# A two-layer encoder: four instead of three seven-product tiles per second matrix, and an adding DMA for their sums

## The chip, the cores and the metric

The kernel runs on one core of one Trainium2 chip. The metric is the device time of one execution in microseconds (us), as the median of several runs; lower is better. The engines are named as in the profile: PE (matmul), PEld (its weight loads), DVE (VectorE), ACT (ScalarE), POOL (GpSimd), SP (SyncE, which here only issues DMAs).

## The reference, cut to what matters

A trunk of two layers on 256 tokens of width 2048, float32. Each layer is an attention (which the change does not touch) and a squared-ReLU MLP with 8192 hidden units, each added to a residual `x`.

```python
def sq_relu_mlp(h, w1, w2):
    return jnp.square(jax.nn.relu(h @ w1)) @ w2      # w1: 2048 x 8192, w2: 8192 x 2048

for i in range(DEPTH):                               # DEPTH = 2
    ...                                              # x = x + attention(rms_norm(x))
    x = x + sq_relu_mlp(rms_norm(x, g), w1, w2)
return rms_norm(x, final_norm)
```

## The kernel before

**Accuracy by parts.** Every float32 operand is cut into a high part (float32r, made by ACT with a cast) and a low part (the rest, made by DVE with a subtraction). One product of two 128-row blocks is three matmuls of 128x512 (high by high, high by low, low by high; lines 196 to 198). The parts of the weights are the tiles `wh` and `wl` (`split`, lines 191 and 192).

**The MLP in groups.** Each of the two MLPs runs in four groups of 2048 hidden units (`ffn`, g = 0 to 3). A group is four calls of `gemm_pair`: two column pairs (cp = 0 and 1) of the first matrix, then two of the second. A column pair multiplies 256 rows by 2048 by 1024 columns. It is eight *steps*; a step takes one pair of 128-row tiles of the left side and one weight block of 512 KB twice (two DMAs on SP's queue).

**Two kinds of step.** An "s" step does the usual eight products (24 matmuls). An "x" step does seven (21 matmuls), by a Strassen-like scheme: DVE first makes sums of the four weight blocks (`prep_x`: tile `sums`, and one block of `w` overwritten), ACT and DVE cut these into `hs` and `ls`, and the left side needs sums of its own, which `sums_and_parts` makes on DVE for each hidden tile pair in `pairs2`. Four of the seven products go into extra PSUM banks ("1", "6", "7", "5"); after the last x step of a column pair, in its last step, `begin` combines them in an SBUF tile `C` (128 x 4 x 512).

**Order of the work.** The order of each engine is the order in which the program is written, step by step; nothing is moved afterwards. While PE multiplies step i, ACT and DVE make the parts of step i+2 (`prep(i + 2, n)` behind quarter n of the step: sums at n = 0, parts of the first half at n = 1, `ls` at n = 2, parts of the second half at n = 3). The pool of `wh` and `wl` has four buffers and a step uses two of each, so the parts of step i+2 go into the buffers of step i and cannot be made earlier than PE lets go of them. Weights are loaded three to five steps ahead into three buffers.

**Between the matrices.** In the second step behind a column pair of the first matrix (for cp = 1 that is the second step of the second matrix), PE transposes the squared hidden values in four rounds r = 0 to 3, each into one of the four extra PSUM banks; ACT and DVE empty each bank into `hT` (a pair not in `pairs2`: cast by ACT, subtraction by DVE at line 192; a pair in `pairs2`: a copy by ACT at line 702, and `sums_and_parts` in a later step). The first x step of the next column pair writes these same banks.

**The residual.** For the second matrix, `put` adds the four standard banks to `x` in the last step (DVE, four of 128x512 from PSUM). `early` adds what stands in `C` to `x` on DVE (one of 128x1024 and two of 128x512) in two later steps of the next column pair, for groups 0 to 2; in group 3 it stands in the last step or near it, because the next norm needs `x`.

The order of the eight steps of a second-matrix column pair, with `pairs2 = (2, 3, 5)`, is s0 s1 x2 s4 x3 s6 x5 s7 in groups 0 to 2.

Of the kernel before, what the change touches and what calls it, by code (L numbers as in the profile page):

```python
# [14 lines left out]
P = 128  # L15
# [32 lines left out]
def tile_encoder(ctx: ExitStack, tc: tile.TileContext, ins, out):  # L48
# [84 lines left out]
    def subtract(engine, out, a, b):  # L133
        engine.tensor_tensor(out=out, in0=a, in1=b, op=ALU.subtract)  # L134
# [143 lines left out]
    QUARTERS = (0, 0), (1, 0), (1, 1), (0, 1)  # L278
    STD = {(0, 0): "2", (0, 1): "3", (1, 0): "4", (1, 1): "S"}

    def gemm_pair(w, cp, A, sums_of, order, finish, split_end=False):
        made, q = [], {}
        first_x = [n for n, o in enumerate(order) if o[0] == "x"]
        touched = set()

        def left(pair, which):

            t, u = A[pair // 2], 2 * (pair % 2)
            if which in ("S2", "S3", "S4"):
                c = sums_of[pair]  # L290
                return [c[:, h, ("S3", "S2", "S4").index(which), :] for h in range(2)]
            a, ts_ = {"A11": (0, 0), "A12": (1, 0), "S1": (0, 1), "A21": (0, 1), "A22": (1, 1)}[which]
            return [t[:, u + a, h, ts_ * P:(ts_ + 1) * P] for h in range(2)]

        def product(bank, a, b, last):
            if not q:
                q.update({k: banks[:, n, :] for k, n in sum_banks().items()})
            three(q[bank], a, b, bank not in touched, last)
            touched.add(bank)

        X = (("1", "A11", 2), ("2", "A12", 3), ("6", "S2", 6), ("7", "S3", 4), ("4", "A22", 0), ("3", "S4", 1),
             ("5", "S1", 5))

        for n, (kind, pair) in enumerate(order):
            k, u = pair // 2, pair % 2
            loads = [(w[k, 2 * cp + c].rearrange("p (a n) -> p a n", n=512)[:, 2 * u:2 * u + 2, :],
                      2 - 2 * c, 4 - 2 * c) for c in (1, 0)]
            if kind == "x":
                def quarter(s, m, pair=pair, n=n):
                    for bank, a, b in X[2 * m:2 * m + 2]:  # L310
                        product(bank, left(pair, a), (s.hi[b], s.lo[b]), n == first_x[-1] and bank in "1567")
            else:
                def quarter(s, m, pair=pair, n=n):
                    tb, c = QUARTERS[m]
                    for kk in range(2):
                        b = 2 * (1 - c) + kk
                        a = (("A11", "A12"), ("A21", "A22"))[tb][kk]
                        product(STD[tb, c], left(pair, a), (s.hi[b], s.lo[b]), n == len(order) - 1 and kk == 1)
            s = Step(kind, loads, quarter)
            s.even = pair % 2 == 0  # L320
            steps.append(s)
            made.append(s)

        if split_end:
            ends = made[-2:]
            for e, s in enumerate(ends):
                def quarter(s, m, e=e):
                    tb, m = m // 2, m % 2
                    pair = order[len(order) - 2 + m][1]
                    for kk in range(2):  # L330
                        b = 2 * (1 - e) + kk
                        a = (("A11", "A12"), ("A21", "A22"))[tb][kk]
                        product(STD[tb, e], left(pair, a), (ends[m].hi[b], ends[m].lo[b]), m == 1 and kk == 1)
                s.quarters = quarter

        def begin(m):
            if m == 0:
                C = q["C"] = part.pool.tile([P, 4, 512], F32, name="C", tag="C")
                nc.scalar.copy(C[:, 0, :], q["1"])
                subtract(nc.vector, C[:, 1, :], q["6"], C[:, 0, :])  # L340
            elif m == 1:
                subtract(nc.vector, q["C"][:, 2, :], q["C"][:, 1, :], q["7"])
            elif m == 2:
                add(nc.vector, q["C"][:, 1::2, :], q["C"][:, 1:3, :], q["5"].unsqueeze(1).to_broadcast([P, 2, 512]))

        s = made[first_x[-1] + 1]
        for m in range(3):
            s.after[0 if s is made[-1] else m].append(lambda m=m: begin(m))
        finish(made, q)
        return made  # L350
# [317 lines left out]
    def ffn(norm, w1, w2, next_norm, next_done):  # L668
        for g in range(4):
            last = g == 3  # L670
            pairs2 = (3, 5) if last else (2, 3, 5)
            hT, sums = [None] * 4, {}

            def hidden(made, q, cp, hT=hT, sums=sums, pairs2=pairs2, last=last):
# [10 lines left out]
                for r in range(4):  # L685
# [10 lines left out]
                    def post(r=r, held=held):  # L696
                        c, half, pair = 2 * cp + r // 2, r % 2, 4 * cp + r
                        if half == 0:
                            hT[c] = opool.tile([P, 4, 2, T], F32R, name="hT", tag="o")
                        if pair in pairs2:  # L700
                            raw = part.pool.tile([P, 2, T], F32, name="h", tag="h", bufs=2)
                            nc.scalar.copy(raw, held["t"])

                            def parts_of(c=c, half=half, raw=raw, pair=pair):
                                sums[pair] = part.pool.tile([P, 2, 3, P], F32R, name="hs", tag="hsum", bufs=3)
                                sums_and_parts(raw, hT[c], half, sums[pair])
                            steps[i + (3 if cp else 2 * r - 1)].after[1].append(parts_of)
                        else:
                            to = hT[c][:, 2 * half:2 * half + 2]
                            split(to[:, :, 0, :], to[:, :, 1, :], held["t"])  # L710
# [11 lines left out]
            def residual(made, q, cp, parted, last=last):  # L722
# [1 line left out]
                    add(nc.vector, to(cp, tb, c), to(cp, tb, c), q[STD[tb, c]])  # L724

                def early(n):
                    C = q["C"]
                    if n == 0:
                        o = x[:, 0, cp * 1024:(cp + 1) * 1024]
                        add(nc.vector, o, o, C[:, 0:2, :].rearrange("p a n -> p (a n)"))  # L730
                    else:
                        subtract(nc.vector, to(cp, 1, 0), to(cp, 1, 0), C[:, 2, :])
                        add(nc.vector, to(cp, 1, 1), to(cp, 1, 1), C[:, 3, :])

                if not parted:
                    i = steps.index(made[-1])
                    for n in range(2):
                        if last:
                            made[-1].after[n].append(lambda n=n: early(n))
                        else:  # L740
                            at_after(i + 4 + 2 * n, 1, lambda n=n: early(n))
                    for m, (tb, c) in enumerate(QUARTERS):
                        made[-1].after[m].append(lambda tb=tb, c=c: put(tb, c))
                    if last:
# [20 lines left out]

            for cp in range(2):
                parted = last and cp == 1
                order = range(8) if last else (0, 1, 2, 4, 3, 6, 5, 7)
                if parted:
                    order = ((0, 1, 2, 4, 3, 5, 6, 7), (0, 1, 3, 2, 5, 4, 6, 7))[next_done is None]  # L770
                gemm_pair(w2g, cp, hT, sums, ff_order(pairs2, order), lambda made, q, cp=cp, parted=parted: residual(made, q, cp, parted),
                          parted)

    ffn(norms[1], ins["ffn0_w1"], ins["ffn0_w2"], lambda: norms[2], begin_norm(2, True))

# [360 lines left out]
```

## Time and profile before

| | |
|---|---|
| median of 3 runs | 2272.35 us (2272.34 to 2273.08) |
| the profiled execution | 2271.95 us, of which the span is 2270.2 us |
| PE busy | 2247.7 us (99%), 10904 matmuls |
| DVE busy | 1876.2 us (83%), 2215 instructions |
| ACT busy | 1263.4 us (56%), 1570 instructions |
| POOL busy | 0.7 us, 6 instructions |
| granted TensorE clock | 0.999 |
| HBM read | 426.38 MB, 189 GB/s over the span |

How to read it: the span runs from the first to the last instruction of the program; the remaining 1.75 us of the execution lie around it. The busy share of an engine is a mean over the attention and the MLPs. In the views "lines", a row is a group of like instructions: source line, engine, operation, tiles out<-in with their shapes, count, then the summed and mean duration, then the idle time of the engine just before them and what ended it. Consecutive instructions of one engine overlap a little, so the distance from start to start, not the duration, is what an instruction occupies; matmuls of 128x512 have a duration of about 0.39 us but follow each other at about 0.227 us.

### The profile page before, as it was taken

How to read it: one execution, taken by the hardware profiler on the slowest of the kernel's cores; microseconds unless marked ns; L12 is line 12 of the kernel's file. 1: busy time of each engine (PE TensorE's matmuls, PEld its weight loads, DVE VectorE, ACT ScalarE, POOL GpSimd, SP SyncE). 2: the span in 40 equal slices, each digit the busy share in tenths (PEclk: the TensorE clock that was granted, in tenths of full speed). 3: DMA queues.
4: the chain of work that ended last, by engine and by line, in shares of the span. 5: the costliest groups of instructions: out<-in, count | busy, mean ns of one | idle time of the engine just before them, and what ended most of it. 6: DMA issues, size and time to landing. Idle time of an engine off the chain costs nothing.

```text
span 2270.2 us, 28396 instructions
## 1 busy us (share of the span) xinstructions
PE 2247.7 (99%) x10904; PEld 1883.7 (83%) x10904; DVE 1876.2 (83%) x2215; ACT 1263.4 (56%) x1570; POOL 0.7 (0%) x6
## 2 busy tenths in 40 slices
PE   8999999999999999999999999999999999999998
PEld 7888888888888888888888888888888888888886
DVE  6777666899999999989877667757999999999988
ACT  6555445665565565565444544456665665664664
POOL 0000000000000000000000000000000000000000
PEclk9999999999999999999999999999999999999999
DMA  7556555556656656655555445544666666656664
GB/s 252 185 177 190 181 178 175 186 186 205 203 186 203 205 185 198 206 179 189 204 176 182 180 167 170 182 168 149 205 198 196 199 193 197 203 189 201 199 214 143
DMA packets 110728, 430.33 MB, mean 190 GB/s; under 512 B 23872, under 2 KB 24448, under 8 KB 92160
## 3 DMA queue, kind: packets, MB, share of 16 engines
q1 hardware_dynamic: 109920, 426.82, 58.0%
q10 hardware_dynamic: 672, 1.70, 0.2%
q8 instruction: 85, 1.39, 0.2%
q14 instruction: 51, 0.42, 0.1%
HBM read 426.38 MB, written 2.10 MB: 189 GB/s over the span
## 4 chain that ended last, share of the span: by engine, by line
PE 91%; DVE 5%; ACT 2%; issue 1%; DMA 0%; SPq 0%; ACTq 0%; DVEq 0%
PE banks L196 23%; PE banks L198 23%; PE banks L197 23%; PE banks L221 13%; PE banks L223 7%; DVE wl L192 2%; PE banks L693 1%; DVE C L137 1%; DVE sums L137 1%; DVE C L134 0%; ACT wh L191 0%; PE banks L379 0%; ACT hs L177 0%; ACT C L679 0%; PE banks L891 0%
## 5 line engine op out<-in xcount | busy, mean ns | idle before, releaser
L192 DVE TENSOR_TENSOR wl<-w,wh 128x1024 fp32r<-128x1024 f32 (+1 forms) x802 | 965.8, 1217 | 294.3 <-ACT wh L191 288.8
L191 ACT CAST wh<-w 128x1024 fp32r<-128x1024 f32 (+1 forms) x802 | 829.6, 1048 | 583.1 <-PE banks L198 338.5
L221 PE MATMUL banks<-xT,wh 128*128 128x512 f32 x1280 | 456.4, 400 | 0.0
L196 PE MATMUL banks<-wh,xT 128*128 128x512 f32 x1104 | 434.9, 394 | 0.0
L198 PE MATMUL banks<-wh,xT 128*128 128x512 f32 x1104 | 430.1, 390 | 0.0
L197 PE MATMUL banks<-wl,xT 128*128 128x512 f32 x1104 | 430.0, 390 | 0.0
L223 PE MATMUL banks<-xT,wl 128*128 128x256 f32 x1280 | 359.0, 280 | 0.0
L196 PE MATMUL banks<-wh,hT 128*128 128x512 f32 x804 | 316.3, 393 | 1.9 <-DVE hT L192 1.9
L198 PE MATMUL banks<-wh,hT 128*128 128x512 f32 x804 | 313.2, 390 | 0.0
L197 PE MATMUL banks<-wl,hT 128*128 128x512 f32 x804 | 313.0, 389 | 0.0
L221 PEld LDWEIGHTS banks<-xT,wh 128*128 128x128 f32 x1280 | 241.2, 188 | 55.8
L198 PEld LDWEIGHTS banks<-wh,xT 128*128 128x128 f32 x1104 | 207.2, 188 | 43.8
L223 PEld LDWEIGHTS banks<-xT,wl 128*128 128x128 f32 x1280 | 242.3, 189 | 0.2
L196 PEld LDWEIGHTS banks<-wh,xT 128*128 128x128 f32 x1104 | 207.4, 188 | 41.0
L197 PEld LDWEIGHTS banks<-wl,xT 128*128 128x128 f32 x1104 | 207.6, 188 | 40.6
L177 ACT CAST hs<-sums 128x1536 fp32r<-128x1536 f32 x92 | 136.6, 1485 | 180.2 <-DVE sums L137 180.2
L196 PEld LDWEIGHTS banks<-wh,hT 128*128 128x128 f32 x804 | 151.0, 188 | 33.3 <-DVE hT L192 3.3
L198 PEld LDWEIGHTS banks<-wh,hT 128*128 128x128 f32 x804 | 150.9, 188 | 31.8
L197 PEld LDWEIGHTS banks<-wl,hT 128*128 128x128 f32 x804 | 151.1, 188 | 30.1
L134 DVE TENSOR_TENSOR ls<-sums,hs 128x1536 fp32r<-128x1536 f32 x92 | 161.1, 1751 | 0.3 <-ACT hs L177 0.3
L137 DVE TENSOR_TENSOR sums<-w 128x1024 f32<-128x1024 f32 x92 | 112.1, 1218 | 0.0
L196 PE MATMUL banks<-wh,oT 128*128 128x512 f32 x192 | 76.5, 399 | 0.0
(188 smaller groups left out, 2289.3 us busy)
## 6 DMA issues: line engine op xcount, KB each, us to landing
w<-in_ffn_w_dram SPq DMA_DIRECT2D x512, 512.0 KB, 4.7
w<-in_dil_wqkv_dram SPq DMA_DIRECT2D x72, 1024.0 KB, 4.8
w<-in_na_wqkv_dram SPq DMA_DIRECT2D x47, 1024.0 KB, 4.9
w<-in_na_wo_dram SPq DMA_DIRECT2D x16, 1024.0 KB, 4.8
w<-in_dil_wo_dram SPq DMA_DIRECT2D x8, 1024.0 KB, 4.7
bias<-in_rpb_dram SPq DMA_DIRECT2D x32, 96.0 KB, 9.9
out_dram<-x SPq DMA_DIRECT2D x8, 256.0 KB, 2.6
x<-in_x_dram SPq DMA_DIRECT2D x3, 512.0 KB, 9.3
```

The lines of the kernel that those rows point to most:

```text
L134: engine.tensor_tensor(out=out, in0=a, in1=b, op=ALU.subtract)
L137: engine.tensor_tensor(out=out, in0=a, in1=b, op=ALU.add)
L177: nc.scalar.copy(s.hs, s.sums)
L191: nc.scalar.copy(dst_hi, src)
L192: nc.vector.tensor_tensor(out=dst_lo, in0=src, in1=dst_hi.bitcast(F32), op=ALU.subtract)
L196: nc.tensor.matmul(o, left[0], right[0], start=start, stop=False)
L197: nc.tensor.matmul(o, left[0], right[1], start=False, stop=False)
L198: nc.tensor.matmul(o, left[1], right[0], start=False, stop=stop)
L221: nc.tensor.matmul(o, s.hi[a][:, cs], xt.rearrange("p h t -> p (h t)"), start=first, stop=False)
L223: nc.tensor.matmul(o[:, :T], s.lo[a][:, cs], xt[:, 0, :], start=False, stop=last)
L693: nc.tensor.transpose(t[:, a, tb * P:(tb + 1) * P], q["C"][:, 2 * tb + f // 4, f % 4 * P:(f % 4 + 1) * P], ident)
```

## The change

In groups 0 to 2 of both MLPs the second matrix gets a fourth pair by seven products (`pairs2 = (2, 3, 5, 6)`), a fourth buffer for the sums of the left side, and other orders: s0 s1 x2 x3 s4 x5 x6 s7 for cp = 0 and s0 x2 x3 s1 x5 s4 x6 s7 for cp = 1. `sums_and_parts` for the hidden pairs 5 and 6 stand in the fourth and fifth step of cp = 0 (before: pair 5 in the fourth). The two `early` additions of these groups go from DVE; in their place one DMA, issued by POOL in the first step of the next column pair, adds the whole of `C` to `x` in SBUF. So that one addition serves all four blocks, `begin` stores its third block negated (`negated=True`, for all second matrices), which makes three DVE instructions into four.

```diff
-    def gemm_pair(w, cp, A, sums_of, order, finish, split_end=False):
+    def gemm_pair(w, cp, A, sums_of, order, finish, split_end=False, negated=False):
...
             elif m == 1:
-                subtract(nc.vector, q["C"][:, 2, :], q["C"][:, 1, :], q["7"])
+                ab = (q["7"], q["C"][:, 1, :]) if negated else (q["C"][:, 1, :], q["7"])
+                subtract(nc.vector, q["C"][:, 2, :], *ab)
+            elif m == 2 and negated:
+                C = q["C"]
+                subtract(nc.vector, C[:, 3, :], q["5"], C[:, 2, :])
+                add(nc.vector, C[:, 1, :], C[:, 1, :], q["5"])
...
-            pairs2 = (3, 5) if last else (2, 3, 5)
+            pairs2 = (3, 5) if last else (2, 3, 5, 6)
...
-                                sums[pair] = part.pool.tile([P, 2, 3, P], F32R, name="hs", tag="hsum", bufs=3)
+                                sums[pair] = part.pool.tile([P, 2, 3, P], F32R, name="hs", tag="hsum", bufs=4)
                                 sums_and_parts(raw, hT[c], half, sums[pair])
-                            steps[i + (3 if cp else 2 * r - 1)].after[1].append(parts_of)
+                            steps[i + (2 + r if cp else 2 * r - 1)].after[1].append(parts_of)
...
                 def early(n):
-                    C = q["C"]
-                    if n == 0:
-                        o = x[:, 0, cp * 1024:(cp + 1) * 1024]
-                        add(nc.vector, o, o, C[:, 0:2, :].rearrange("p a n -> p (a n)"))
-                    else:
-                        subtract(nc.vector, to(cp, 1, 0), to(cp, 1, 0), C[:, 2, :])
-                        add(nc.vector, to(cp, 1, 1), to(cp, 1, 1), C[:, 3, :])
+                    o = x[:, n, cp * 1024:(cp + 1) * 1024]
+                    add(nc.vector, o, o, q["C"][:, 2 * n:2 * n + 2, :].rearrange("p a n -> p (a n)"))
+
+                def bring():
+                    nc.gpsimd.dma_start(x[:, :, cp * 1024:(cp + 1) * 1024],
+                                        q["C"].rearrange("p (t a) n -> p t (a n)", t=2), accum_op=ALU.add)
 
                 if not parted:
                     i = steps.index(made[-1])
-                    for n in range(2):
-                        if last:
+                    if last:
+                        for n in range(2):
                             made[-1].after[n].append(lambda n=n: early(n))
-                        else:
-                            at_after(i + 4 + 2 * n, 1, lambda n=n: early(n))
+                    else:
+                        at_after(i + 1, 1, bring)
...
-                order = range(8) if last else (0, 1, 2, 4, 3, 6, 5, 7)
+                order = range(8) if last or not cp else (0, 2, 3, 1, 5, 4, 6, 7)
...
                 gemm_pair(w2g, cp, hT, sums, ff_order(pairs2, order), lambda made, q, cp=cp, parted=parted: residual(made, q, cp, parted),
-                          parted)
+                          parted, negated=True)
```

Where this moves DVE's instructions, first place: the last step of cp = 0 of a second matrix, group 0. Before, the combining of `C`, the four additions to `x`, and the parts of an s step (two `wl`) stand here, and the next step's x sums follow:

```order
L134 TENSOR_TENSOR C<-banks,C 128x512
L134 TENSOR_TENSOR C<-C,banks 128x512
L137 TENSOR_TENSOR C<-C,banks 128x2x512
L137 TENSOR_TENSOR x<-x,banks 128x512 x2
L192 TENSOR_TENSOR wl<-w,wh 128x1024
L137 TENSOR_TENSOR x<-x,banks 128x512 x2
L192 TENSOR_TENSOR wl<-w,wh 128x1024
L137 TENSOR_TENSOR sums<-w 128x1024
```

In the changed kernel the same step holds the preparation of an x step (three additions into `sums` and `w`, two `wl`, one `ls`), laid between the additions to `x`:

```order
L134 TENSOR_TENSOR C<-banks,C 128x512 x3
L137 TENSOR_TENSOR C<-C,banks 128x512
L137 TENSOR_TENSOR x<-x,banks 128x512
L137 TENSOR_TENSOR sums<-w 128x1024
L137 TENSOR_TENSOR sums<-sums,w 128x512
L137 TENSOR_TENSOR w<-sums,w 128x512
L137 TENSOR_TENSOR x<-x,banks 128x512
L192 TENSOR_TENSOR wl<-w,wh 128x1024
L137 TENSOR_TENSOR x<-x,banks 128x512
L134 TENSOR_TENSOR ls<-sums,hs 128x1536
L137 TENSOR_TENSOR x<-x,banks 128x512
L192 TENSOR_TENSOR wl<-w,wh 128x1024
```

So x2 of cp = 1 is prepared one step earlier, in the step that also ends cp = 0.

Second place: DVE in the second step of cp = 0 of a second matrix, where the transposed hidden values are emptied from their banks (`hT<-banks`). Before, behind the last `wl` of x2's preparation (first row), the emptying of round 0 comes at once, between the parts of an s step:

```order
L192 TENSOR_TENSOR wl<-w,wh 128x1024
L192 TENSOR_TENSOR hT<-banks,hT 128x2x256
L192 TENSOR_TENSOR wl<-w,wh 128x1024
L192 TENSOR_TENSOR hT<-banks,hT 128x2x256 x2
L192 TENSOR_TENSOR wl<-w,wh 128x1024
L137 TENSOR_TENSOR sums<-w 128x1024
L137 TENSOR_TENSOR sums<-sums,w 128x512
```

In the changed kernel the sums of x3 stand ahead of it:

```order
L192 TENSOR_TENSOR wl<-w,wh 128x1024
L137 TENSOR_TENSOR sums<-w 128x1024
L137 TENSOR_TENSOR sums<-sums,w 128x512
L137 TENSOR_TENSOR w<-sums,w 128x512
L192 TENSOR_TENSOR hT<-banks,hT 128x2x256
L192 TENSOR_TENSOR wl<-w,wh 128x1024
L134 TENSOR_TENSOR ls<-sums,hs 128x1536
L192 TENSOR_TENSOR hT<-banks,hT 128x2x256
L192 TENSOR_TENSOR wl<-w,wh 128x1024 x3
```

What moved: three additions now stand between x2's last `wl` and the first `hT<-banks`, and of the three emptyings by DVE two are left (round 2 is now a copy by ACT).

## The prediction

> **What bounds the kernel now.** I read the page first, then the windows of one group, then DVE's timeline step by step. The page's busy line:
>
> ```profile
> PE 2247.7 (99%) x10904; PEld 1883.7 (83%) x10904; DVE 1876.2 (83%) x2215; ACT 1263.4 (56%) x1570; POOL 0.7 (0%) x6
> ```
>
> PE is busy throughout, so fewer matmuls are worth time. But 83% for DVE is a mean over attention and MLPs. Here are four windows from the second group of the first MLP on: cp = 0 and cp = 1 of a second matrix, then cp = 0 and cp = 1 of the next first matrix; the columns are the window's length, then busy time of PE, PEld, DVE, ACT, POOL.
>
> ```profile
> 658.92:703.37 44.45, 43.88 (x201) 35.88 (x200) 41.13 (x47) 28.68 (x34) 0.00 (x0) 1.00 0.62 194
> 703.37:744.85 41.48, 41.48 (x185) 34.36 (x184) 38.42 (x39) 21.51 (x20) 0.00 (x0) 1.00 0.67 213
> 744.85:786.33 41.48, 41.48 (x185) 34.36 (x184) 38.43 (x39) 21.49 (x20) 0.00 (x0) 1.00 0.64 199
> 786.33:829.90 43.57, 43.57 (x200) 35.81 (x199) 40.44 (x48) 29.57 (x36) 0.00 (x0) 1.00 0.58 183
> ```
>
> DVE works 41.13 of 44.45 us where the change adds to it: 3.3 us are free there, and 3.1 in the next window. The clock is full (1.00). What matters then is how far DVE may fall behind PE. I cut PE's stream into steps of 24 or 21 matmuls; the first three of cp = 0:
>
> ```profile
> 658.92:664.36 5.44, 5.44 (x25) 4.50 (x24) 5.44 (x8) 4.50 (x6) 0.00 (x0) 1.00 0.54 189
> 664.36:672.77 8.41, 7.84 (x42) 6.08 (x41) 6.83 (x8) 6.99 (x10) 0.00 (x0) 1.00 0.42 125
> 672.77:677.53 4.76, 4.76 (x22) 3.89 (x23) 4.73 (x6) 2.72 (x4) 0.00 (x0) 1.00 0.72 229
> ```
>
> An s step takes 5.44 us (24 matmuls, 0.227 each), an x step 4.76 (21), and the second step 8.41 because it holds the transposes. Now DVE's timeline from the parts of s1 to the emptying of the first transposes (start, duration, line, operation, and in brackets idle time before it):
>
> ```profile
> 662.60 1.22 DVE L192 TENSOR_TENSOR wl<-w,wh 128x1024 fp32r<-128x1024 f32 x1
> 663.74 1.22 DVE L137 TENSOR_TENSOR sums<-w 128x1024 f32<-128x1024 f32 x1
> 664.99 0.69 DVE L137 TENSOR_TENSOR sums<-sums,w 128x512 f32<-128x512 f32 x1
> 665.72 0.69 DVE L137 TENSOR_TENSOR w<-sums,w 128x512 f32<-128x512 f32 x1
> 666.33 1.22 DVE L192 TENSOR_TENSOR wl<-w,wh 128x1024 fp32r<-128x1024 f32 x1
> 667.46 1.75 DVE L134 TENSOR_TENSOR ls<-sums,hs 128x1536 fp32r<-128x1536 f32 x1
> 670.73 1.23 DVE L192 TENSOR_TENSOR wl<-w,wh 128x1024 fp32r<-128x1024 f32 x1 [1.51 <-ACT wh L191]
> 671.87 0.68 DVE L192 TENSOR_TENSOR hT<-banks,hT 128x512 fp32r<-128x512 f32 x1
> 672.47 1.22 DVE L192 TENSOR_TENSOR wl<-w,wh 128x1024 fp32r<-128x1024 f32 x1
> ```
>
> By starts, an x step's preparation occupies DVE for 2.59 (three additions) + 1.13 + 1.67 (`ls`, 1.75 less 0.08 of overlap) + 1.14 = 6.53 us, against 4.76 to 5.44 of PE's time; an s step's takes two `wl`, 2.27. I call *lag* how long after the end of PE's step i DVE ends its work of that step. The work of the step that ends at 658.92 ends at 663.82: lag 4.9. The preparation of x2 ends at 671.96, and its PE step at 664.36: lag 7.6. No PE stall follows, because the step between is 8.41 long. So DVE already trails PE by about a step, and only x-free stretches bring it back. How much lag is allowed shows in PE's rows of x2:
>
> ```profile
> 672.61 0.50 PE L196 MATMUL banks<-wh,hT 128*128 128x512 f32 x1 [0.31 <-DVE hT L192]
> ...
> 674.34 0.39 PE L197 MATMUL banks<-ls,hs 128*128 128x512 f32 x1
> ```
>
> PE first needs `ls` 1.73 us into the x step, and behind `ls` DVE has one more `wl` (1.14): the lag may reach the length of the step between plus some 2.7 us, so 7.4 before an x step that follows an x step, 8.1 when an s step lies between. The other two tiles of the step (`wl` at once and `wl` in the second half) give 0.2 more.
>
> **The change part by part.** Removed from PE: two column pairs x three groups x two MLPs = 12 x steps in place of s steps, 3 matmuls each: 36 x 0.227 = 8.2 us, all on the path (PE 99%). That is 1.36 us a group, for six groups.
>
> Added to DVE per group: two x preparations for s ones, 2 x (6.53 - 2.27) = 8.5 us; one `sums_and_parts` for one emptying of 0.60 (671.87 to 672.47). This is its cost, from its first to its last instruction and the next one:
>
> ```profile
> 682.46 0.28 DVE L134 TENSOR_TENSOR c<-h 128x128 f32<-128x128 f32 x1
> ...
> 685.26 2.36 DVE L192 TENSOR_TENSOR wl<-w,wh 128x1024 fp32r<-128x1024 f32 x2 [0.29 <-ACT wh L191]
> ```
>
> 2.5 us, 2.8 with the wait for ACT behind it: +1.9. The combining of `C`, the additions to `x`, and the idle time ahead of them:
>
> ```profile
> 698.53 1.22 DVE L192 TENSOR_TENSOR wl<-w,wh 128x1024 fp32r<-128x1024 f32 x1 [0.98 <-ACT wh L191]
> 699.67 0.68 DVE L134 TENSOR_TENSOR C<-banks,C 128x512 f32<-128x512 f32 x1
> 700.39 0.69 DVE L134 TENSOR_TENSOR C<-C,banks 128x512 f32<-128x512 f32 x1
> 701.18 1.22 DVE L137 TENSOR_TENSOR C<-C,banks 128x1024 f32<-128x1024 f32 x1
> 702.32 1.28 DVE L137 TENSOR_TENSOR x<-x,banks 128x512 f32<-128x512 f32 x2
> 703.51 1.22 DVE L192 TENSOR_TENSOR wl<-w,wh 128x1024 fp32r<-128x1024 f32 x1
> 704.65 1.27 DVE L137 TENSOR_TENSOR x<-x,banks 128x512 f32<-128x512 f32 x2
> 705.85 1.22 DVE L192 TENSOR_TENSOR wl<-w,wh 128x1024 fp32r<-128x1024 f32 x1
> ```
>
> Combining takes 2.65 and, as four instructions of 128x512, 0.72 + 0.79 + 0.72 + 0.60 = 2.83; the four additions 2.39. The 0.98 us idle is DVE waiting for buffers that PE still holds: the lag cannot fall under the 1.8 us that this row leaves (699.75 against 697.93, where PE's x5 ends: 677.53 and two s and two x steps).
>
> Taken from DVE: the `early` additions, twice per group.
>
> ```profile
> 723.25 1.22 DVE L137 TENSOR_TENSOR x<-x,C 128x1024 f32<-128x1024 f32 x1
> 724.38 1.22 DVE L192 TENSOR_TENSOR wl<-w,wh 128x1024 fp32r<-128x1024 f32 x1
> ...
> 733.45 0.68 DVE L134 TENSOR_TENSOR x<-x,C 128x512 f32<-128x512 f32 x1
> 734.05 0.68 DVE L137 TENSOR_TENSOR x<-x,C 128x512 f32<-128x512 f32 x1
> 734.65 3.86 DVE L192 TENSOR_TENSOR wl<-w,wh 128x1024 fp32r<-128x1024 f32 x3
> ```
>
> 1.13 + 1.20 = 2.33, twice 4.7 us. Net, DVE gets 8.5 + 1.9 + 0.4 - 4.7 = 6.1 us more per group. But the relief lies in the middle of cp = 1 and in the next first matrix, where DVE waits for buffers anyway; the load lies in cp = 0 and at the seam to cp = 1. So I follow the lag through the steps (after each: lag + work - PE's step).
>
> Step s0 is as before: lag 7.6. Step s1: the sums of x3 now stand ahead of the first `hT<-banks`. The row at 672.61 shows that x2's first product waits for exactly that instruction (the bank of round 0), so PE now waits 2.59 us more: **first stall 2.6**. The step becomes 11.0 long; work 6.53 + 2 x 0.60: lag 7.6 + 7.7 - 11.0 = 4.3. Step x2: + 2.27 - 4.76 = 1.8, the floor. Step x3 (prepares x5, with pair 5's `sums_and_parts`): + 6.53 + 2.8 - 4.76 = 6.4, allowed 8.1. Step s4 (prepares x6, with pair 6's): + 9.3 - 5.44 = 10.3, allowed 7.4: **second stall 2.9**, lag 7.4. Steps x5 and x6 prepare s steps: 4.9, then 2.4. Step s7: combining 2.83, additions 2.39, and x2 of cp = 1, 6.53, less 5.44: 8.7, allowed 8.1: **third stall 0.6**. Step s0 of cp = 1 prepares x3: 8.1 + 1.1 = 9.2, allowed 7.4: **fourth stall 1.8**. After that 4.9, 6.7 (allowed 8.1), 3.5, 5.3, 2.1: none. Sum 7.9 us a group, times six 47.4, less 8.2: +39.2 us.
>
> Edits without a price on the path: the `early` addition of group 3 as one of 128x1024 for two of 128x512 (0.07 less, twice in all) and the fourth combining instruction there; `bufs=4` (memory only). ACT gets two casts of `hs` a group; it has 15.8 us free in the first window.
>
> The 12 DMAs that add 1 MB each: issued by POOL, which does nothing else then, so nothing queues behind its wait for DVE and ACT. The next readers are the combining that reuses `C` (four x and two s steps between, 29.9 us) and an addition to the same half of `x` in the next group. No row shows such a DMA. The nearest are the weight loads and one 1 MB load among them:
>
> ```profile
> w<-in_ffn_w_dram SPq DMA_DIRECT2D x512, 512.0 KB, 4.7
> gf<-in_final_norm_dram ACTq DMA_DIRECT2D x1, 1024.0 KB, 7.3
> ```
>
> Reading two operands could double 7.3 to 14.6 us, under 29.9: hidden, price 0. Below nothing it cannot go, since DVE's relief is already counted. Above, it can make weight loads late by 7.3 - 4.7 = 2.6 us, at most 12 x 2.6 = 31 us; I take 0: with three buffers a load starts when the parts of the step three before are made, so it has the time of two preparations, here x3's and s1's, 6.53 + 2.27 = 8.8 us, for its 4.7. The Trainium skill, "SBUF — State Buffer", section "Who interferes with whom", has a rule that speaks against a DMA from POOL: GpSimd writes its descriptors through a port pair that it shares with VectorE, under an exclusive lock, and the loser waits for a whole instruction; a `tensor_tensor` with two SBUF inputs takes only the read side. By that rule these additions and subtractions delay no descriptor and the sum stays as it is; if the lock did bite, the DMA would be late, not DVE, by DVE instructions of 1.75 us at most. No run here shows it yet.
>
> The sum against the profiled execution: 2271.95 + 39.2 = 2311.2 us; the median of the runs lies 0.4 higher: 2311.6, forecast 2311.
>
> **The rivals.**
> (1) DVE's free time covers it: faster. A group has 12.6 us of DVE idle time (3.3 + 3.1 + 3.1 + 3.1 in the four windows), more than the 6.1 added. If work could be done ahead into that time, PE keeps 8.2 us: 2263.8. For it: the sum over a group fits. Against it: the floor row, where DVE waits because PE holds the buffers; work cannot be drawn ahead by more than about a step. It decides if the stalls of a group stay under 1.36 us; the first alone is 2.6.
> (2) Only the bank wait is real, and lag is tolerated because I place PE's needs too early: 6 x 2.6 - 8.2 = +7.4, 2279.4. For it: no PE stall by lag is to be seen before, so the allowed 7.4 is read from one step. Against it: it would take 3 us more patience at three places.
> (3) The adding DMAs hold up the weight loads, beside the forecast: 12 x 0 to 2.6 us on top, 2311 to 2342, middle 2327. For it: the DMA engines' share is 0.62 to 0.67 here. Against it: the 8.8 us.
>
> **How the numbers follow.** Forecast 70% (its own range 2290 to 2330: each of three lag stalls may be off by 1 us, 6 x 3 = 18 to each side); rival 1 8%; rival 2 10%; rival 3 12%. The range 2278 to 2334 leaves out rival 1, the upper half of rival 3 and the tails. About 0.2% (4.5 us) can be told from no change. Faster: rival 1. Within 0.2%: rival 2 with a half of the bank wait, 5%. Slower: the rest, 87%.
>
> **What would show it.** Matmuls 10868. In the windows of a second matrix: cp = 0 near 48 us and cp = 1 near 42, with DVE over 95% busy in cp = 0; first-matrix windows unchanged. The waits should list PE or PEld on `hT` L197 of the new kernel, on `ls` and on `wl`, together some 47 us. Now stands there only:
>
> ```profile
> PEld banks L196 <- DVE hT L192: 6.3, 14, 0.6
> ```
>
> The chain of waits should lead through DVE in cp = 0. POOL's DMAs should land in under 15 us with nobody waiting. Wrong would be: PE without waits in x2, x6 and at the seam (rival 1), waits on `hT` alone (2), or ACT waiting on a weight DMA (3).

## The result, and the profile after

The changed kernel takes 2328.70 us (median of 4 runs, 2328.31 to 2329.26), the kernel before 2272.72 beside it: ratio 1.0248, 95% interval 1.0235 to 1.0260, so 56.0 us slower. The profiled execution has a span of 2326.6 us.

The engines' busy line, and the new DMA beside a load of the same size in the list of issues (count, KB, median us from issue to landing):

```profile
PE 2267.4 (97%) x10868; PEld 1888.6 (81%) x10868; DVE 1910.4 (82%) x2269; ACT 1281.7 (55%) x1594; POOL 15.2 (1%) x18
w<-in_dil_wqkv_dram SPq DMA_DIRECT2D x72, 1024.0 KB, 4.8
...
x<-C POOLq DMA_DIRECT2D x12, 1024.0 KB, 12.9
```

36 matmuls are gone, as the change says, and yet PE's busy time rose by 19.7 us: the same matmuls ran slower. The windows of the second group (cp = 0 and 1 of the second matrix, then of the next first matrix) show where. The columns are as in the prediction; the 1.00 or 0.97 behind POOL is the granted clock:

```profile
669.59:720.39 50.80, 45.23 (x198) 36.29 (x196) 47.28 (x57) 30.96 (x37) 0.00 (x0) 0.97 0.51 168
720.39:763.40 43.01, 41.76 (x181) 33.48 (x180) 40.06 (x41) 22.33 (x21) 1.20 (x1) 1.00 0.73 229
763.40:804.88 41.48, 41.48 (x184) 34.36 (x183) 36.24 (x36) 21.44 (x20) 1.20 (x1) 1.00 0.75 231
804.88:848.46 43.58, 43.58 (x200) 35.84 (x199) 40.45 (x48) 29.54 (x36) 0.00 (x0) 1.00 0.58 179
```

The first matrix's windows are as before (41.48 and 43.57); cp = 0 went from 44.45 to 50.80 and cp = 1 from 41.48 to 43.01. DVE's relief shows in the third window (36.24 for 38.43 us), where nobody waits for DVE. In the first it is busy for 47.28 of 50.80 us.

PE's waits in the list of waits (us in total, times, longest):

```profile
PE banks L196 <- DVE hT L192: 17.4, 6, 2.9
PE banks L197 <- DVE wl L192: 11.8, 12, 1.2
PE banks L196 <- ACT wh L191: 9.8, 6, 1.7
```

Six waits for `hT` are the first stall, six for `wh` with six of the twelve for `wl` the second (x6), the other six for `wl` the fourth (x3 of cp = 1). Together 39 us. Before, PEld's 6.3 us stood there, which the prediction shows, and this row of PE, which it does not:

```profile
PE banks L196 <- DVE hT L192: 1.9, 6, 0.3
```

The second group shows the first two stalls one by one: x2's first product, then x6's first two.

```profile
685.87 0.50 PE L196 MATMUL banks<-wh,hT 128*128 128x512 f32 x1 [2.90 <-DVE hT L192]
...
707.57 0.51 PE L196 MATMUL banks<-wh,hT 128*128 128x512 f32 x1 [1.64 <-ACT wh L191]
708.82 0.79 PE L197 MATMUL banks<-wl,hT 128*128 128x512 f32 x1 [0.75 <-DVE wl L192]
```

DVE's timeline shows what the first is made of: x3's three additions stand between the last `wl` of x2 and the `hT` that PE waits for.

```profile
681.40 1.23 DVE L192 TENSOR_TENSOR wl<-w,wh 128x1024 fp32r<-128x1024 f32 x1 [1.52 <-ACT wh L191]
682.55 1.22 DVE L137 TENSOR_TENSOR sums<-w 128x1024 f32<-128x1024 f32 x1
683.80 0.69 DVE L137 TENSOR_TENSOR sums<-sums,w 128x512 f32<-128x512 f32 x1
684.52 0.69 DVE L137 TENSOR_TENSOR w<-sums,w 128x512 f32<-128x512 f32 x1
685.13 0.68 DVE L192 TENSOR_TENSOR hT<-banks,hT 128x512 fp32r<-128x512 f32 x1
```

ACT's timeline shows how the second begins: the `wh` that x6's first product waits for stands in ACT's queue behind two casts for pair 6, and these wait for DVE's `sums_and_parts`.

```profile
705.40 0.62 ACT L457 CAST hT<-h 128x512 fp32r<-128x512 f32 x1 [5.13 <-DVE h L134]
706.05 0.51 ACT L458 CAST hs<-c 128x384 fp32r<-128x384 f32 x1
706.47 1.04 ACT L191 CAST wh<-w 128x1024 fp32r<-128x1024 f32 x1
```

**The term that the forecast did not have** is in three windows of 3.41 us around x6:

```profile
705.09:708.50 3.41, 1.34 (x5) 0.56 (x3) 2.98 (x6) 3.07 (x4) 0.00 (x0) 1.00 0.50 197
708.50:711.91 3.41, 3.09 (x7) 2.48 (x8) 3.26 (x4) 3.41 (x5) 0.00 (x0) 0.50 0.00 0
711.91:715.33 3.42, 3.42 (x16) 2.78 (x15) 3.31 (x3) 1.64 (x2) 0.00 (x0) 1.00 0.63 190
```

In the first PE works 1.34 us, the rest is the wait. In the next the granted clock is 0.50: from 708.82 on PE has its weights, but the window holds 7 matmuls where the one behind it holds 16. At x2 of the same group the wait of 2.90 us falls half into one such window and half into the next, and the clock stays full:

```profile
681.20:684.61 3.41, 1.77 (x10) 1.25 (x8) 3.14 (x4) 1.69 (x4) 0.00 (x0) 1.00 0.24 56
684.61:688.02 3.41, 2.15 (x9) 1.78 (x10) 3.41 (x4) 3.41 (x5) 0.00 (x0) 1.00 0.69 251
688.02:691.44 3.42, 3.42 (x16) 2.83 (x16) 3.42 (x4) 2.38 (x3) 0.00 (x0) 1.00 0.10 10
```

The trace has ten such stretches inside the MLPs' second matrices, 40.96 us at half clock; before there was none.

### The profile page after: what moved, and what is told of

Its sections match the earlier page's. It is cut to its first block, busy times and chain, and to the rows that moved or that the text cites. A ratio compares the mean times of both kernels' runs of the same rounds, so it can differ in the third digit from the quotient of the medians.

```text
span 2326.6 us, 28439 instructions
## 1 busy us (share of the span) xinstructions
PE 2267.4 (97%) x10868; PEld 1888.6 (81%) x10868; DVE 1910.4 (82%) x2269; ACT 1281.7 (55%) x1594; POOL 15.2 (1%) x18
## 4 chain that ended last, share of the span: by engine, by line
PE 80%; DVE 13%; ACT 3%; issue 3%; DMA 0%; ACTq 0%; SPq 0%; DVEq 0%
PE banks L197 20%; PE banks L196 20%; PE banks L198 19%; PE banks L221 13%; PE banks L223 6%; DVE wl L192 4%; DVE sums L137 3%; ACT wh L191 1%; DVE ls L134 1%; DVE w L137 1%; DVE C L134 1%; DVE C L137 1%; PE banks L698 1%; ACT hs L177 1%; DVE x L137 1%
## 5 line engine op out<-in xcount | busy, mean ns | idle before, releaser
L196 PE MATMUL banks<-wh,hT 128*128 128x512 f32 x744 | 296.8, 399 | 27.3 <-DVE hT L192 17.4
L197 PE MATMUL banks<-wl,hT 128*128 128x512 f32 x744 | 295.2, 397 | 11.8 <-DVE wl L192 11.8
L198 PE MATMUL banks<-wh,hT 128*128 128x512 f32 x744 | 294.0, 395 | 0.0
L177 ACT CAST hs<-sums 128x1536 fp32r<-128x1536 f32 x104 | 154.2, 1482 | 193.7 <-DVE sums L137 193.7
L198 PEld LDWEIGHTS banks<-wh,xT 128*128 128x128 f32 x1104 | 207.2, 188 | 43.5
L196 PEld LDWEIGHTS banks<-wh,hT 128*128 128x128 f32 x744 | 141.4, 190 | 59.6 <-DVE hT L192 18.9
L134 DVE TENSOR_TENSOR ls<-sums,hs 128x1536 fp32r<-128x1536 f32 x104 | 182.2, 1752 | 2.2 <-ACT hs L177 1.6
L197 PEld LDWEIGHTS banks<-wl,hT 128*128 128x128 f32 x744 | 141.7, 191 | 44.5 <-DVE wl L192 16.4
L198 PEld LDWEIGHTS banks<-wh,hT 128*128 128x128 f32 x744 | 142.0, 191 | 29.5
L137 DVE TENSOR_TENSOR sums<-w 128x1024 f32<-128x1024 f32 x104 | 126.7, 1218 | 13.5 <-DMA w<-in_ffn_w_dram 13.5
## 6 DMA issues: line engine op xcount, KB each, us to landing
x<-C POOLq DMA_DIRECT2D x12, 1024.0 KB, 12.9
```

Source lines behind the costliest of these rows:

```text
L137: engine.tensor_tensor(out=out, in0=a, in1=b, op=ALU.add)
L177: nc.scalar.copy(s.hs, s.sums)
L196: nc.tensor.matmul(o, left[0], right[0], start=start, stop=False)
L197: nc.tensor.matmul(o, left[0], right[1], start=False, stop=False)
L198: nc.tensor.matmul(o, left[1], right[0], start=False, stop=stop)
```

## The experiments

Two theories stood. The *ledger* theory: DVE's backlog, as the prediction counts it, makes the waits, and a wait that leaves PE idle for most of a 3.41 us window makes the next window run at half clock. Against it: the adding DMA; or the clock falling for a reason of its own.

**Is it the DMA?** One run takes the DMA out of the changed kernel, another puts it alone into the kernel before.

```diff
-                        at_after(i + 1, 1, bring)
+                        for n in range(2):
+                            at_after(i + 4 + 2 * n, 1, lambda n=n: early(n))
```

> The changed kernel with the sums added to x by DVE again (two instructions, in the fourth and sixth step of the next column pair) instead of the adding DMA. Theory (the DMA is hidden and the steps in which DVE adds have lag to spare): no change beyond 3 us, 2326 to 2332. Rival (the adding DMA delays the weight loads and so PE): up to 12 x 1.1 = 13 us faster, 2315.

Measured 2326.34 us (ratio 1.0231, 1.0216 to 1.0247): the slowdown stays without the DMA. The second run keeps three x steps and the old orders, with `bring` and `negated` alone:

> Three x steps and the orders of the kernel before, with only the adding DMA (and the negated block that it needs) in place of DVE's additions. Theory (the DMA costs PE nothing, and DVE's 4.7 us a group were not on the path): the time of the kernel before, 2271 to 2274. Rival (the DMA disturbs the weight loads): 12 x 1 to 2.6 us slower, 2284 to 2303.

Measured 2273.34 us against 2273.07: ratio 1.0000 (0.9991 to 1.0010). The DMA and the relief of DVE are worth nothing by themselves. It does disturb: in the lists of waits ACT waits for weight loads for 44.5 us in the changed kernel, 28.6 with the DMA alone, and 7.2 in the changed kernel without it, in this order:

```profile
ACT wh L191 <- DMA w<-in_ffn_w_dram: 44.5, 24, 4.2
```

```profile
ACT wh L191 <- DMA w<-in_ffn_w_dram: 28.6, 15, 3.2
```

```profile
ACT wh L191 <- DMA w<-in_ffn_w_dram: 7.2, 8, 2.4
```

But ACT has the time: with the DMA alone PE loses nothing, and in the changed kernel only x5 of cp = 1 is late, by 0.0 to 0.4 us.

**Is the first stall the additions ahead of `hT`, and what does a wait cost?** Three runs put nothing but additions to a scratch tile at that place into the kernel before: 1.2, 2.6 and 5.2 us of DVE.

```diff
+                def fill():
+                    f = part.pool.tile([P, 1024], F32, name="fill", tag="fill")
+                    add(nc.vector, f, x[:, 0, 0:1024], x[:, 0, 0:1024])
+                    add(nc.vector, f[:, 0:512], f[:, 0:512], f[:, 512:1024])
+                    add(nc.vector, f[:, 512:1024], f[:, 0:512], f[:, 512:1024])
+                if cp and not last:
+                    at_after(i + 1, 0, fill)
```

> The kernel before with three additions of the shapes of an x step's sums (128x1024, 128x512, 128x512: 2.6 us of DVE, on a tile that nothing else reads) ahead of the emptying of the transposes' banks, in groups 0 to 2 of both MLPs. Theory (PE waits for that emptying, and where PE is idle for over about 2.2 us of a clock window of 3.41 us, the next window runs at half clock): 6 x 2.3 to 2.6 us of waits and 2 to 4 half windows of 1.7 us lost each: 2272.7 + 14 to 16 + 3 to 10, 2289 to 2299, with half-clock rows in the clock of this run. Rival (DVE's order there does not matter): 2273. Rival (waits alone, no clock): 2287 to 2288 with a full clock.

> The kernel before, with one more addition of 128x1024 on VectorE ahead of the emptying of the first banks of transposes of a group's second matrix (some 1.2 us, against the 2.6 us of three such additions that cost 23.7 us in all). Theory (a wait costs its own length, and a further 1.6 to 1.7 us only if it leaves TensorE idle for more than about 2 us within one window of 3.4 us): six waits of 1.1 to 1.25 us, no stretch at half clock, 2279 to 2281 us at the clock of the kernel before. Rival (any wait of TensorE here is followed by half clock): 6 x 1.7 = 10 us more, 2289 to 2291 us. Rival (VectorE has slack there for 1.2 us): 2273 us.

> The kernel before, with six more additions of 128x1024 on VectorE at the same place, 5.2 us by twice the 2.6 us of three. Theory: six waits of 5.2 us (31 us) and after every one of them at least one stretch at half clock (a wait of 5.2 us has at least 2.6 us in one of two windows of 3.4 us), sometimes two: 2272.7 + 31 + 10 to 25 = 2314 to 2329 us. Rival (waits alone, the clock's fall being chance): 2304 us.

Measured 2296.41, 2280.12 and 2317.19 us (ratios 1.0100, 1.0030, 1.0191; intervals 1.0085 to 1.0115, 1.0018 to 1.0042, 1.0176 to 1.0206). PE's wait for `hT` in the lists of waits, in the order 1.2, 2.6, 5.2:

```profile
PE banks L196 <- DVE hT L192: 8.7, 6, 1.5
```

```profile
PE banks L196 <- DVE hT L192: 17.4, 6, 2.9
```

```profile
PE banks L196 <- DVE hT L192: 33.7, 6, 5.6
```

The middle row is that of the changed kernel to the digit, so the three additions are enough for the whole first stall. Each fill lengthens the step by its own length (1.1, 2.6, 5.3 us), 7, 15 and 32 us in all. The rest is the clock: with 1.2 us there is no stretch at half clock and the kernel is 6.8 us slower; with 2.6 us there are 17.07 us at half clock, with 5.2 us 37.55, and 8 and 12 us come on top.

**Can the first stall be emptied away?** The banks' emptying goes ahead of x3's preparation, in the changed kernel.

```diff
+            if i in empty_first:
+                for pe, post in s.tasks[n]:
+                    post()
...
-                post()
+                if i not in empty_first:
+                    post()
```

> The changed kernel, but in the second step of cp = 0 of a second matrix the banks of the transposes are emptied ahead of the preparation of x3, not behind its three additions. Theory (DVE's backlog sets the end, and a wait only moves it): the wait of PE at the start of x2 (2.6 us, six times, and the half clock behind it, some 9 us in all) goes, but DVE is then 2.6 us further behind PE at x5 and x6, so the waits there grow by about as much; only the half clock of x2 is saved, and the time falls by 0 to 10 us, to 2319 to 2329. Rival (each wait stands alone): 6 x 2.6 + 9 = 25 us saved, 2304.

Measured 2321.68 us (ratio 1.0212, 1.0195 to 1.0229), 7 us under the changed kernel. The step before x2 is 8.25 us again, but x2 now waits for ACT's raw copies, which stand behind `hs`, which waits for DVE's additions; and x5 waits 0.7 us longer (its step takes 7.23 for 6.56). PE's new wait in the list:

```profile
PE banks L196 <- ACT h L708: 9.0, 6, 1.5
```

The work moved in the queue is late elsewhere: the backlog is kept.

**Is the fourth stall two x steps in a row on a high lag?** cp = 1 gets the order of cp = 0.

```diff
-                order = range(8) if last or not cp else (0, 2, 3, 1, 5, 4, 6, 7)
+                order = range(8)
```

> The kernel after, with the second sweep's steps in the order of the first sweep (s0 s1 x2 x3 s4 x5 x6 s7 in place of s0 x2 x3 s1 x5 s4 x6 s7). Theory (VectorE's backlog, by the same ledger as the prediction): in the second sweep VectorE then ends its work 4.1 to 7.0 us behind TensorE, under the 7.4 us that the pools allow, so the stall at x3 of that sweep (1.8 us a group) goes: 6 x 1.8 to 2.1 = 11 to 13 us less than the kernel after, 2316 to 2318 us. Rival (that stall isn't due to two x in a row with the s between them missing): 2328 us; or a new wait at x6 of that sweep: 2322 to 2328 us.

Measured 2315.87 us (ratio 1.0187, 1.0172 to 1.0202), 12.8 us under the changed kernel. In all six groups cp = 1 lasts 40.80 us, which is four s steps of 5.44 and four x steps of 4.76 with no wait at all. Of PE's twelve waits for `wl` six are left, those at x6 of cp = 0:

```profile
PE banks L197 <- DVE wl L192: 4.6, 6, 0.8
```

A lag that the ledger puts at up to 7.0 is tolerated there; 9.2, in the order of the changed kernel, cost 1.8.

**Is the second stall DVE's work?** `ls` of x5 and x6 is left out in cp = 0.

```diff
+        elif n == 2 and getattr(s, "no_ls", False):
+            for a in range(3):
+                s.hi[4 + a] = s.lo[4 + a] = s.hs[:, a, :]
```

> The kernel after, but in the sweep over the first half of the block rows x5 and x6 bring no low parts of their block sums (the kernel's high parts are used in their place), which takes 1.67 us of VectorE from each of the two preparations; those low parts are left out of the result. Theory (VectorE's backlog): TensorE's wait at x6's first product falls from 2.9 us to nothing, and the stretch at half clock that follows it goes too; some 0.6 us may show at the seam instead: 6 x 2.9 = 17 us and 6 x 1.7 = 10 us less than the kernel after, 4 us back at most, so 2300 to 2311 us. Rival (the second stall comes from ScalarE or from the loads that the adding DMAs delay, not from VectorE's work): 2326 to 2329 us. Second rival (the wait goes but the clock stays as low): 2311 to 2314 us.

Measured 2319.93 us (ratio 1.0202, 1.0185 to 1.0219): the expectation missed. The stall went from 2.8 to 2.1 us, and five of six kept their stretch at half clock. I had counted both `ls`, but x6's stands behind x6's first product; and of x5's 1.67 us DVE spent 1.10 waiting, in this row of DVE's timeline:

```profile
876.88 1.23 DVE L195 TENSOR_TENSOR wl<-w,wh 128x1024 fp32r<-128x1024 f32 x1 [1.10 <-ACT wh L194]
```

That `wh` stands behind `hs` (1.48 us) in ACT's queue. So a later run, on top of that one, casts `hs` last:

```diff
+            if getattr(s, "no_ls", False):
+                nc.scalar.copy(s.hs, s.sums)
```

> The kernel without the low parts of the block sums of x5 and x6 in the first sweep (those low parts are left out of the result, as in the run before of this kind), and with the cast of these two sums (hs, 1.48 us of ScalarE) put behind the cast of the last two blocks (wh) in place of ahead of it. Theory (taking 1.67 us from VectorE ahead of x6's first product shortened the wait by 0.73 us only, because VectorE then idled 1.10 us for a wh that stood behind hs on ScalarE): the other 0.94 us a group comes too, the wait at x6 falls to some 1.2 us, under what lowers the clock, and the five stretches at half clock there go: 2319.9 - 6 x 0.94 - 5 x 1.65 = 2306 us, 2304 to 2312. Rival (what is left of the stall there comes from neither, but from the time at which ScalarE could begin x5's casts): 2318 to 2321 us.

Measured 2307.41 us (ratio 1.0154, 1.0138 to 1.0171). x6's first product now waits for nothing, the second still 0.76 us for `wl`, and no stretch at half clock is left at x6:

```profile
878.14 0.45 PE L202 MATMUL banks<-wh,hT 128*128 128x512 f32 x1
879.35 0.50 PE L203 MATMUL banks<-wl,hT 128*128 128x512 f32 x1 [0.76 <-DVE wl L198]
```

The second stall is a chain DVE, ACT, DVE in which both queues' orders count, not a sum of DVE's durations alone.

**Is it the waiting that lowers the clock?** The first try put eight matmuls into bank "6" ahead of x2:

> The kernel after, with eight matmuls of 128x512 more ahead of the first product of x2 in the first sweep of each of the six groups: they go to a bank that x2 starts afresh right behind them, and take weights that are there, so TensorE works for 8 x 0.227 = 1.8 us of the 2.55 us that it waits at this place. Nothing else is changed; 48 matmuls are added and none taken away. Theory (the missing 18.9 us is the clock that falls when TensorE idles for some 2 us of a window of 3.4 us): the wait for hT stays as long from end to end, some 0.7 us of it idle, and the stretches at half clock behind it go, which cost 2.87, 0 and 1.6 us in the three groups of a pass, 9 us in both: 2318 to 2322 us. Rival (the clock falls for another reason, such as the load on the chip): 2327 to 2330 us. Rival (the added matmuls come on top): 2328.7 + 6 x 1.8 = 2339 us.

Measured 2342.73 us (ratio 1.0308, 1.0292 to 1.0323). It tested nothing: bank "6" is one that the transposes had filled, and the added matmuls waited for ACT to empty it, so that they ran when the wait was over, here at half clock:

```profile
505.37 3.78 PE L312 MATMUL banks<-wh 128*128 128x512 f32 x8 [3.57 <-ACT h L710]
```

The second try adds zeros to a bank already in use:

```diff
+                    if negated and not cp and m == 0 and len(first_x) == 4:
+                        for _ in range({2: 9, 6: 6}.get(n, 0)):
+                            nc.tensor.matmul(q["2"], zeros, s.hi[2] if n == 2 else made[5].hi[5], start=False, stop=False)
```

> The kernel after, with matmuls that add nothing (weights of zero, into a bank that is in use already, operands that are there long before) where TensorE waits in the first sweep: nine of 128x512 ahead of x2's first product (9 x 0.227 = 2.0 of the 2.9 us that it idles there), six ahead of x6's (1.36 of 1.65 us). 90 matmuls are added, 20.4 us of TensorE, none is taken away, and in the built program none of the 90 waits for anything. Theory (the missing 18.9 us is the clock, which falls when TensorE idles for some 1.9 us or more of one window of 3.4 us): the waits end when they did, the ten stretches at half clock go, and up to 0.6 us a group may show at the seam, where half clock had let VectorE catch up: 2328.7 - 18.9 = 2310 us, 2308 to 2315. Rival (the clock falls for another reason): 2327 to 2330 us. Rival (the added matmuls come on top): 2349 us.

Measured 2318.95 us (ratio 1.0205, 1.0188 to 1.0222), 9.8 us under the changed kernel with 90 matmuls more. They filled the wait, x2's first product came as late as before, and no stretch at half clock is left:

```profile
501.55 2.33 PE L314 MATMUL banks<-wh,zeros 128*128 128x512 f32 x9
504.71 0.50 PE L198 MATMUL banks<-wh,hT 128*128 128x512 f32 x1 [0.82 <-DVE hT L194]
```

```profile
666.55:716.38 49.83, 47.55 (x212) 37.86 (x211) 46.65 (x56) 30.98 (x37) 0.00 (x0) 1.00 0.52 169
716.38:760.25 43.87, 42.25 (x181) 33.40 (x180) 40.52 (x42) 22.16 (x21) 1.20 (x1) 1.00 0.72 228
```

That settles the clock's cause. The gain is 9.8 and not the 18.9 us expected, because a slow PE is also a PE that DVE can catch up with: at full clock x6 has a new wait, for its `ls`, and takes 0.7 us more, and the seam, x3 and x5 of cp = 1 cost 0.3, 0.2 and 0.2 us more. PE's row of the new wait:

```profile
529.53 0.50 PE L199 MATMUL banks<-ls,hs 128*128 128x512 f32 x1 [0.25 <-DVE ls L136]
```

**Can the additions go to the idle GpSimd?**

```diff
+            if n == 2 and i + 3 < len(steps) and getattr(steps[i + 3], "pool_sums", False):
+                x_sums(steps[i + 3], nc.gpsimd)
```

> The kernel after, with the three additions that form the block sums of x2 and x5 in the first sweep (3.85 us of VectorE each) given to GpSimd, one step earlier; x3 and x6 keep theirs on VectorE. No trace here has such an addition on GpSimd. Theory A (the two engines don't disturb each other; GpSimd has the work done in time): 2 x 3.85 us a group are off VectorE, the waits at x2 and x6 (2.55 and 2.9 us) and the half clock behind them go: 2328.7 - 6 x 5.45 - 18.9 = 2277 us, 2275 to 2290. Theory B (an addition on GpSimd stops VectorE's two-input instructions for as long as it runs, so that the work is on VectorE's path still, and longer): 2325 to 2345 us. Between the two: GpSimd's sums come late, or stop VectorE for part of the time: 2290 to 2325 us.

Measured 2321.58 us (ratio 1.0218, 1.0202 to 1.0233): between the two theories, nearer to the second. POOL's timeline and DVE's of the same stretch:

```profile
684.59 2.41 POOL L137 TENSOR_TENSOR sums<-w 128x1024 f32<-128x1024 f32 x1 [10.08 <-DVE ls L134]
687.07 2.15 POOL L137 TENSOR_TENSOR sums<-sums,w 128x512 f32<-128x512 f32 x1
689.30 2.15 POOL L137 TENSOR_TENSOR w<-sums,w 128x512 f32<-128x512 f32 x1
```

```profile
684.97 7.57 DVE L197 TENSOR_TENSOR wl<-w,wh 128x1024 fp32r<-128x1024 f32 x3
```

Three `wl`, 3.86 us in a row of the prediction, take 7.57 while GpSimd adds: DVE loses 3.7 us, more than it was spared, since the three additions are 2.59 us of DVE in the prediction's rows (the 3.85 of the expectation is not their sum). One by one the three are:

```profile
684.97 3.10 DVE L197 TENSOR_TENSOR wl<-w,wh 128x1024 fp32r<-128x1024 f32 x1
688.00 2.31 DVE L197 TENSOR_TENSOR wl<-w,wh 128x1024 fp32r<-128x1024 f32 x1
690.23 2.31 DVE L197 TENSOR_TENSOR wl<-w,wh 128x1024 fp32r<-128x1024 f32 x1
```

Each `wl` ends 1.1 us behind the end of one of GpSimd's additions (687.00, 689.22, 691.45), and GpSimd's second and third end 1.1 to 1.2 us behind the end of a `wl` (688.07, 690.31). So the two engines work in turns, and each waits for the whole of the other's instruction. The Trainium skill, "SBUF — State Buffer", "Who interferes with whom", says that a VectorE instruction with two SBUF inputs contends with a GpSimd instruction that reads SBUF, and that the loser blocks for the whole instruction; these rows agree. The first stall fell from 2.6 to 1.2 us, the second stayed (1.7 us at x6's first product in four groups, 3.3 in two). Why the first fell is not shown; the sums of x2 are made a step earlier here.

No kernel here is faster than the kernel before; of those with the fourth x pair that leave nothing of the work out, the best is the one with cp = 1 in plain order, 2315.87.

## Why the prediction came out as it did

The sign, the places and three of four sizes of the stalls were right; what PE waits for at x6 and at x3 of cp = 1 was not, and a term was missing. The lengths of the steps, from the first matmul of one to that of the next, give each stall as a mean over six groups (us per group; the last column is the kernel with the zero matmuls, which has full clock throughout):

| step of the prediction | forecast | changed kernel | at full clock |
|---|---|---|---|
| first stall (x2, `hT`) | 2.6 | 2.56 | 2.56 |
| second stall (x6) | 2.9 | 2.84 | 2.84 + 0.69 |
| third stall (seam) | 0.6 | 0 | 0.30 |
| fourth stall (x3 of cp = 1) | 1.8 | 1.81 | 1.99 |
| late loads (x5 of cp = 1) | 0 | 0.18 | 0.42 |
| half clock | no term | 3.2 | 0 |
| sum | 7.9 | 10.6 | 8.8 |
| times 6, less 8.2 for the matmuls | +39.2 | +55.3 | +44.6 |
| measured | | +56.0 | +46.2 |

- *The 36 matmuls, 8.2 us*: gone as forecast, 10868 left.
- *First stall*: 2.6 and 2.56; shown by putting the same 2.6 us into the kernel before. (The step before x2 takes 8.25 us in the kernel before; the prediction's window of 8.41 ends 0.16 us behind x2's first product.)
- *Second stall*: the size was right, the reasoning too simple. It was counted as DVE's work with PE waiting for `ls`. PE waits for ACT's `wh` and for `wl`; `ls` shows only at full clock, with 0.69 us more; and over half of what was taken from DVE went into waiting for ACT. The prediction's own rows have such a wait, 1.51 us within the lag of 7.6. So 2.84 against 2.9 is in part luck.
- *Third stall*: none in the changed kernel, since x6's half clock gives DVE the time. At full clock it is 0.30 us. The kernel with eight matmuls has both cases: the four groups whose x6 ran at full clock have it (0.3 us), the two with half clock there don't.
- *Fourth stall*: 1.8 and 1.81; it went when the order of cp = 1 was changed, as the ledger says. Here too PE waits for `wl` and not for `ls`.
- *The DMA, priced 0*: 12.9 us to landing (forecast under 15), no time lost by itself. The sign that the prediction named for rival 3 did appear, ACT waiting on a weight DMA, for 37 us more than without the adding DMA. But ACT is idle half of the time, and only 0.18 us a group reaches PE, so rival 3's price did not come. Its middle, 2327, lies nearer to the 2328.7 than the forecast does, but without the DMA the kernel still takes 2326.34.
- *The windows*: cp = 0 near 48 us and cp = 1 near 42 were forecast, 50.7 to 53.8 and 42.6 to 43.0 measured. The prediction's own stalls add up to more than it wrote: 44.45 - 0.68 + 2.6 + 2.9 = 49.3 and 41.48 - 0.68 + 0.6 + 1.8 = 43.2. At full clock they measure 49.8 and 43.5, so only the rest of cp = 0 is the half clock. DVE is busy for 93% of cp = 0, not over 95%: it waits for ACT in between. PE's waits in the list add up to 39 us, not to some 47.
- *Rival 1 and rival 2* fell with the first rows of the list of waits: PE waits at x2, x6 and in cp = 1.
- *The missing term*: the prediction wrote "the clock is full (1.00)" and priced a wait at its own length. Half clock took 3.2 us a group (the excess of x2 over 4.90 and of x6 over 4.76 + 1.03), 19 us in all; without it the kernel is 9.8 us faster, so that is what it costs net.
- *Smaller slips*: 1.73 + 1.14 is 2.87 and not some 2.7, by which the ledger's sum would be 7.6 us a group for 7.9. The upper bound 2334 leaves out a quarter of rival 3's span, not its upper half.

The forecast 2311 thus is near 2319, what the kernel with the zero matmuls takes at full clock; of the 8 us between them, the 0.9 us a group between the two sums of the table are 5.4, and under 3 us I have not placed. That the 2328.7 lies inside the forecast's own range, 2290 to 2330, is in part luck: its width was meant for errors of 1 us in each of three lag stalls. None was that large, and a term that the prediction did not have took up the room.

## What to carry to other kernels

Ask not whether an engine has idle time over a group of steps but how far it may fall behind at each step: in the changed kernel's four windows DVE is idle for 14.8 us in all, and PE still waits for it, since the buffers let no work be done ahead by more than about a step. Keep such a ledger by the rows of one step's preparation, with the other engines' queue orders in it. And price a wait of PE at more than its length once it fills 55 to 60% of a window of 3.41 us: here 2.6 us cost 3.9.

## What the runs showed of the hardware

- **The clock falls after one window that is mostly idle.** The stretches at half clock lie on a grid of 3.41 us. Over the changed kernel and the eleven runs that followed with waits in PE, every window in which PE's gaps (starts over 1.2 us apart, less 0.227 each) add up to 2.05 us or more is followed by one at half clock, and none with less than 1.85 is, save some that ran at half clock themselves; between the two, both occur. The Trainium skill, "TensorE: Matmul & The Clock Gate", section "HAM oscillation — how this bites in real kernels", gives the rule to avoid idle gaps of over about 3.4 us. The length of the window agrees with these rows; the rule is too mild for them, since waits of 1.64 and 0.75 us in one window were enough.
- **Where a wait falls in the grid decides.** In the changed kernel x2's wait of 2.90 us cost nothing more in the second group, where two windows share it; the wait of 2.91 us in the third, which ends at 864.75, was followed by half clock from 865.52 on. That may be why runs of one kernel can spread more once it waits (2322.8 to 2328.3 for the kernel without the DMA, against 2272.3 to 2274.4 for the one with the DMA alone); it is not shown, and the runs of the changed kernel lie within 1 us.
- **Matmuls that compute nothing can save time**: 90 of them made the kernel 9.8 us faster.
- **An adding DMA of 1 MB within SBUF** landed in 12.9 us, where a load of 1 MB landed in 4.8.
- **GpSimd's additions and DVE's subtractions of two SBUF tiles run in turns.** GpSimd took 2.4 us for 128x1024, against 1.22 on DVE. Beside it a `wl` of 1.22 us took 2.3 to 3.1, and GpSimd's own additions of 128x512 took 2.2 us, of which, by the ends above, some 1.1 are waiting for DVE (an estimate from these rows). DVE's `C<-C,banks`, with one input from PSUM, took no longer beside them: two in 1.27 us.
